# A planner that keeps an account of the engines' queues, and attention by query tile of both key heads

## The chip, the cores and the metric

The kernel runs on one core of one Trainium2 chip. The metric is the device time of one execution in microseconds (us), the median of the runs. Times in the trace are counted from the start of the span, the first instruction of the program in the profile.

## What is computed

The reference is the trunk of an encoder with two layers, in float32. Two sequences go through it with the same weights: the prompt (512 tokens, width 1024) and the sample (256 tokens).

```python
def mixer(h, lp, rope):
    z = h @ lp["w_mix_in"]
    ...
    o_lru = rglru_mixer(xb, yb, lp)
    o_rwkv = rwkv_mixer(zr, lp)
    o_att = attention(q, k, v, lp["attn_q_norm"], lp["attn_k_norm"], rope)
    o = jnp.concatenate([o_lru, o_rwkv, o_att], axis=-1).astype(h.dtype)
    return o @ lp["w_mix_out"]

def layer(x, c, lp, rope):
    mod = (jax.nn.silu(c) @ lp["w_ada"] + lp["b_ada"])[:, None, :]
    sh1, sc1, g1, sh2, sc2, g2, sh3, sc3, g3 = jnp.split(mod, N_MOD, axis=-1)
    h = rmsnorm(x, lp["norm_g"][0]) * (1 + sc1) + sh1
    x = x + 0.5 * g1 * swiglu(h, lp["ffn_w_in"][0], lp["ffn_w_out"][0])
    h = rmsnorm(x, lp["norm_g"][1]) * (1 + sc2) + sh2
    x = x + g2 * mixer(h, lp, rope)
    h = rmsnorm(x, lp["norm_g"][2]) * (1 + sc3) + sh3
    x = x + 0.5 * g3 * swiglu(h, lp["ffn_w_in"][1], lp["ffn_w_out"][1])
    return x
```

Attention has six query heads on two key heads (three query heads each), with 64 numbers a head. For every key head and each of its query heads it computes the scores q times k, a softmax over all tokens, and the product with v.

## The kernel before

Activations lie transposed, features on the partitions and tokens along the free axis. A token block is the whole sequence: 512 columns for the prompt, 256 for the sample. So the same matmul has a moving operand of 512 columns for the one and 256 for the other, and by that a row of the trace tells whose it is.

The dense work is the two feed-forward blocks of each layer and the mixer's two projections. Their weights come by DMA (`wr`), are split by ScalarE and VectorE into a high part `wh` (L270) and a rest `wl` (L271), and every product is three matmuls: `wh` with the high part of the activation, `wh` with its rest, `wl` with its high part (`mm3`). Names of their outputs: `pg` and `pu` (gate and up of the prompt), `pb` (both, of the sample), `ops` (the second matmul of the block, and `wmo`, the mixer's output projection, with `xo` as its input), `mip` (the mixer's input projection).

The small work is the rest. `ssp` is a norm's sum. Attention: `S` (scores), `ptp` (transposes of the probabilities P), `avp` (product with v). The recurrent mixer: `gps`. The RWKV mixer, for one pair of heads after the other: `up` and `ap` (low-rank gates), `kkp` and `bp` (sums over a head), `scps` (scores in chunks, from `AR`, `BK` and `B`), `btps` and `vtps` (transposes), then four levels of `yps` and `dps` (an inverse, in blocks of 32), `u0p`, the chunk recurrence `zps`, `saps`, `stps`, and the output `ywp`, `yp`, `gp`. `adaps` is the modulation. Many of these use a part of the 128 by 128 array, and a row of the trace says which: 64*128 is a half of the rows, 128*64 a half of the columns. A float32 matmul is two records in the trace (two passes), a transpose and a dense matmul are one.

Only TensorE's order is set by the kernel; the other engines' order comes from the framework. The planner is `Sched`. Each sequence's layers are a dense thread, a generator; attention, the recurrent mixer, RWKV and the modulation are small threads. A thread issues its instructions up to a `yield`. Each matmul moves the planner's clock `t` on by a fixed cost (512 columns divided by 2.4 GHz, and so on). What the thread yields is the time after which its next step may be issued, and that is a number written by hand for each place and each of the two sequences, in the table `LAT`:

```python
LAT = {... 'PREP': (5.0, 8.2), 'OP': (1.47, 0.82), ... 'A2': (2.0, 2.1), ... 'R3': (0.68, 0.99), 'R4': (1.8, 6.2), ...}
```

`step` sets `th.ready = self.t + r`. `run` takes a small thread that is ready, if the debt of small work allows it, else the dense thread of the lowest `prio`. In RWKV, `R3` stands between `yps` and `dps` and `R4` between `dps` and the next `yps`; `OP` and `PREP` stand in the preparation from `up` to `scps`. A dense thread yields 0.0 every two of its steps along the contraction (`EV`), so it is always ready, its inputs and weights or not.

An attention unit is (j, qt, hh): one of three query heads, one tile of 128 queries, one of the two key heads. Head `hh` lies on partitions 64 * hh to 64 * hh + 63. `stA` issues one `S` of 128 queries by all keys, and the softmax on VectorE and ScalarE. `stB` issues the transposes of P and the copy to PT, `stC` the product with v into the half `hh` of `avp`. A round of the loop issues `stA` of unit u, `stC` of u - 2 and `stB` of u - 1, then yields `A2`.

## Time and profile before

| | us |
|---|---|
| median of 3 runs (3454.62 to 3456.97) | 3456.47 |
| the profiled execution, its own time | 3462.16 |
| its span | 3459.2 |
| TensorE busy | 3341.5 |
| VectorE busy | 2003.2 |
| ScalarE busy | 1448.2 |
| GpSimd busy | 512.1 |

The span reaches from the first to the last instruction. The difference of 3.0 us from the profiled execution's time lies around it. Busy times are unions of an engine's records, and the end of a matmul's record is modelled, so consecutive records overlap; what a matmul costs in a stream is the distance of the starts.

### The profile page before, as it was taken

To read this page: it belongs to the slowest core of one execution; us is meant where nothing else is said; L and a number is where in the kernel's file an instruction comes from. 1 tells how busy PE (TensorE), PEld (TensorE's weight loads), DVE (VectorE), ACT (ScalarE), POOL (GpSimd) and SP (SyncE) were. 2 spreads that over 40 slices of the span, in tenths; PEclk is the share of its full clock that TensorE was granted. 3 is DMA by queue.
4 is the path that set the end of the run, shared out by engine and by line. 5 is a ranking of instruction groups with operands and counts; after the bars stand their busy time and mean duration, and the time that the engine had idled before them with its cause. 6 is when DMAs were issued, how large, how long until landed. Compare 5 with 4: busy or idle time off the path is not lost. (4 is left out here: it accounts for less than half of the span.)

```text
span 3459.2 us, 69173 instructions
## 1 busy us (share of the span) xinstructions
PE 3341.5 (97%) x28052; PEld 2734.0 (79%) x28052; DVE 2003.2 (58%) x3973; ACT 1448.2 (42%) x2730; POOL 512.1 (15%) x659
## 2 busy tenths in 40 slices
PE   7999999999899899999999999999899999999999
PEld 5777776678877777888888876788789978778899
DVE  4433365775776745546333476667557776446466
ACT  3322243644346433434333346534345564334354
POOL 1100020212221211111000111212211111111010
PEclk9999999999999999999999999999899999999999
DMA  7666674133342222423332331233245533223455
GB/s 276 219 206 208 203 270 145 57 104 113 100 153 93 83 80 83 132 90 119 92 98 86 119 114 62 79 110 102 82 161 164 179 106 108 63 91 125 138 177 161
DMA packets 151630, 445.80 MB, mean 129 GB/s; under 512 B 16912, under 2 KB 20752, under 8 KB 151312
## 3 DMA queue, kind: packets, MB, share of 16 engines
q1 hardware_dynamic: 151312, 441.39, 40.2%
q8 instruction: 220, 3.60, 0.4%
q14 instruction: 98, 0.80, 0.1%
HBM read 427.17 MB, written 14.16 MB: 128 GB/s over the span
## 5 line engine op out<-in xcount | busy, mean ns | idle before, releaser
L270 ACT ACTIVATE wh<-wr 128x512 fp32r<-128x512 f32 (+1 forms) x1368 | 816.6, 602 | 1572.1 <-PE ops L148 485.5
L271 DVE TENSOR_TENSOR wl<-wr,wh 128x512 fp32r<-128x512 f32 (+1 forms) x1368 | 907.3, 668 | 800.4 <-ACT wh L270 769.8
L148 PE MATMUL ops<-an,wh 128*128 128x512 f32 (+1 forms) x2816 | 717.8, 345 | 19.3 <-ACT an L351 7.3
L148 PEld LDWEIGHTS ops<-an,wh 128*128 128x128 f32 x2816 | 480.1, 190 | 99.1 <-issue 13.5
L148 PE MATMUL pb<-xn,wh 128*128 128x256 f32 x2816 | 525.1, 287 | 0.5 <-issue 0.5
L148 PE MATMUL ops<-an,wl 128*128 128x512 f32 (+1 forms) x1408 | 477.2, 339 | 0.1
L148 PE MATMUL pg<-xn,wh 128*128 128x512 f32 x1408 | 449.5, 400 | 7.8 <-ACT xn L417 5.9
L148 PEld LDWEIGHTS pb<-xn,wh 128*128 128x128 f32 x2816 | 433.6, 189 | 19.2 <-issue 11.2
L148 PE MATMUL pu<-xn,wh 128*128 128x512 f32 x1408 | 447.4, 399 | 0.0
L352 POOL TENSOR_TENSOR an<-sg,an 128x512 fp32r<-128x512 f32 (+1 forms) x176 | 192.3, 1093 | 1674.0 <-ACT an L351 1613.0
L148 PE MATMUL pb<-xn,wl 128*128 128x256 f32 x1408 | 396.4, 282 | 4.8 <-DVE wl L271 3.8
L431 DVE SCALAR_TENSOR_TENSOR x<-ops,gat,x 128x256 f32<-128x256 f32 (+1 forms) x352 | 215.8, 614 | 196.0 <-PE ops L148 190.6
L148 PE MATMUL mip<-xn,wh 128*128 128x512 f32 (+1 forms) x1216 | 314.2, 348 | 9.3 <-DVE f L583 2.9
L148 PEld LDWEIGHTS pg<-xn,wh 128*128 128x128 f32 x1408 | 260.1, 188 | 75.6 <-ACT xn L417 6.5
L148 PEld LDWEIGHTS pu<-xn,wh 128*128 128x128 f32 x1408 | 260.1, 188 | 65.5 <-issue 6.6
L148 PEld LDWEIGHTS ops<-an,wl 128*128 128x128 f32 x1408 | 267.0, 190 | 31.6 <-DVE wl L271 0.3
L148 PE MATMUL pg<-xn,wl 128*128 128x512 f32 x704 | 277.4, 394 | 0.0
L148 PE MATMUL pu<-xn,wl 128*128 128x512 f32 x704 | 276.8, 393 | 0.0
L148 PEld LDWEIGHTS pb<-xn,wl 128*128 128x128 f32 x1408 | 265.9, 189 | 6.0 <-DVE wl L271 4.8
L148 PEld LDWEIGHTS mip<-xn,wh 128*128 128x128 f32 x1216 | 208.2, 192 | 48.9 <-issue 12.3
L148 PE MATMUL mip<-xn,wl 128*128 128x512 f32 (+1 forms) x608 | 207.2, 341 | 0.0
L148 PEld LDWEIGHTS pg<-xn,wl 128*128 128x128 f32 x704 | 132.9, 189 | 30.7
(257 smaller groups left out, 3738.5 us busy)
## 6 DMA issues: line engine op xcount, KB each, us to landing
wr<-in_wfi_dram SPq DMA_DIRECT2D x352, 512.0 KB, 3.6
adaw<-in_wada_dram SPq DMA_DIRECT2D x128, 512.0 KB, 4.4
wr<-in_wfo_dram SPq DMA_DIRECT2D x192, 256.0 KB, 2.7
wr<-in_wfo_dram SPq DMA_DIRECT2D x128, 320.0 KB, 2.9
wr<-in_wmi_dram SPq DMA_DIRECT2D x76, 512.0 KB, 3.6
wr<-in_wmo_dram SPq DMA_DIRECT2D x32, 512.0 KB, 3.5
adaw<-in_wadh_dram SPq DMA_DIRECT2D x32, 256.0 KB, 5.2
xsp<-x SPq DMA_DIRECT2D x8, 512.0 KB, 3.6
```

What stands on the lines that cost most here:

```text
L148: PE.matmul(out, lhsT, rhs, start=start, stop=stop, skip_group_check=True)
L270: A.activation(out=hi[:, :n], in_=raw, func=AF.Copy)
L271: V.tensor_tensor(out=lo[:, :n], in0=raw, in1=hi[:, :n].bitcast(F32), op=ALU.subtract)
L352: eng.tensor_tensor(out=lo, in0=src, in1=hi.bitcast(F32), op=ALU.subtract)
L431: V.scalar_tensor_tensor(out=q.x[m], in0=ps, scalar=gat[l][:, i, m, q.i:q.i + 1], in1=q.x[m], op0=ALU.mult, op1=ALU.add)
```

## The change

The change puts an account of the engines' queues in place of the table. VectorE, ScalarE and GpSimd are wrapped (`Engine`): each instruction that the kernel issues there also enters `Model.op`, which gives it a duration by engine, operation and length, starts it once its inputs are written and its output buffer is free, and puts it into the first hole of that engine's queue that holds it (`place`). A matmul waits in the account for its operands, costs 0.4531 ns a column if dense, and 0.1 us more where dense and small work change places (`SWITCH`). The DMA of a weight takes 3.4 us (`DMAT`). A thread that yields a number over zero is now ready 0.05 us after the last instruction of its step ends in the account; one that yields `At(t)` is ready at `t`. A dense thread yields before every second step of the contraction until two inputs (and, at each fourth, the weights) are due. Small threads also wait until the account has a PSUM buffer free for them.

Attention becomes one unit for each (j, qt), with both key heads: two `S` one after the other on different rows of the array, both transposes, and the products with v alternating between the halves of the columns. Scores, transposes and product now are three steps with a yield behind each. The pool `small` has 7 buffers instead of 5, since a unit holds two P. P is overwritten by its transpose instead of a tile PT.

```diff
+SWITCH = 0.1
+DMAT = 3.4
...
+        self.mo.step_last = 0.0
...
+        elif isinstance(r, At):
+            th.ready = r.t
+        elif r > 0 and self.mo.step_last > 0:
+            th.ready = self.mo.step_last + 0.05
...
+            bank = self.mo.bank("m")
+            now = [th for th in act if max(th.ready, 0.0 if th.dense else bank) <= self.t + 1e-9]
             if not now:
-                self.t = min(th.ready for th in act)
+                self.t = min(max(th.ready, 0.0 if th.dense else bank) for th in act)
...
+class Engine:
+
+    def __init__(self, real, m, kind):
+        self.real, self.m, self.kind, self.iv = real, m, kind, []
+
+    def __getattr__(self, name):
+        call = getattr(self.real, name)
+
+        def run(*args, **kw):
+            r = call(*args, **kw)
+            aps = [a for a in args if hasattr(a, "dtype") and hasattr(a, "shape")]
+            outs = [kw[k] for k in ("out", "accum_out") if kw.get(k) is not None]
+            ins = [v for k, v in kw.items() if k not in ("out", "accum_out") and hasattr(v, "dtype") and hasattr(v, "shape")]
+            if "out" not in kw:
+                outs, aps = outs + aps[:1], aps[1:]
+            self.m.op(self, name, outs, ins + aps, kw)
+            return r
+
+        return run
+
+    def place(self, t0, dur):
+        iv = self.iv
+        k = len(iv)
+        while k > 0 and iv[k - 1][1] > t0:
+            k -= 1
+        s = t0
+        while k < len(iv) and iv[k][0] < s + dur:
+            s = max(s, iv[k][1])
+            k += 1
+        iv.insert(k, (s, s + dur))
+        if len(iv) > 400:
+            del iv[:200]
+        return s + dur
...
+    def op(self, e, name, outs, ins, kw):
+        n = 1
+        for a in outs[:1] + ins:
+            z = 1
+            for d in list(a.shape)[1:]:
+                z *= d
+            n = max(n, z)
+        t0 = self.ready(*ins)
+        for a in outs:
+            t0 = max(t0, self.free.get(self.keys(a)[0][0], 0.0))
+        if e.kind == "V":
+            if name == "tensor_tensor_scan":
+                d, lag = 0.1 + 2.15e-3 * n, 0.08
+            elif name == "tensor_scalar":
+                d, lag = 0.1 + 0.66e-3 * n, 0.08
+            elif name == "scalar_tensor_tensor":
+                d, lag = 0.1 + 1.08e-3 * n, 0.08
+            else:
+                d, lag = 0.08 + 1.03e-3 * n, 0.08
+            lag += 0.03
+        elif e.kind == "A":
+            d, lag = 0.11 + 0.83e-3 * n, 0.1
+            if kw.get("accum_out") is not None:
+                d += 0.2
+        else:
+            d, lag = (0.03 + 1.2e-3 * n if name == "memset" else 0.15 + (2.7e-3 if name == "tensor_scalar" else 2.05e-3) * n), 0.06
+        t = e.place(t0 + 0.06, d) + lag
+        for a in outs:
+            for k in self.keys(a):
+                self.w[k] = max(self.w.get(k, 0.0), t) if name != "memset" else max(self.w.get(k, 0.0), t)
+        for a in ins + outs:
+            nm = self.keys(a)[0][0]
+            r = self.r.get(nm, 0.0)
+            self.r[nm] = t if r >= 1e9 else max(r, t)
+        self.step_last = max(self.step_last, t)
+        return t
...
+    def mm(self, out, ins, cost, old):
+        t = self.sch.t
+        need = max(self.ready(*ins), self.free.get(self.keys(out)[0][0], 0.0))
+        if need > t + 0.02:
+            self.stalls.append((t, need - t, out.tensor.name, [a.tensor.name for a in ins if self.ready(a) >= need - 1e-6]))
+            t = need
+        dense = ins[1].dtype == F32R
+        if dense != self.dense:
+            t += SWITCH
+            self.dense = dense
+        t += cost
+        self.sch.t = t
+        for k in self.keys(out):
+            self.w[k] = t + 0.14
+        for a in ins:
+            nm = self.keys(a)[0][0]
+            self.r[nm] = max(self.r.get(nm, 0.0), t)
+        self.r[self.keys(out)[0][0]] = 1e9
...
+    def bank(self, tag):
+        names = self.ring.get(tag, [])
+        t = min((self.r.get(z, 1e9) for z in names), default=0.0)
+        return 0.0 if t >= 1e9 or len(names) < 4 else t
...
+    V, A, G, PE = Engine(nc.vector, mo, "V"), Engine(nc.scalar, mo, "A"), Engine(nc.gpsimd, mo, "G"), nc.tensor
...
-    sm = ctx.enter_context(tc.tile_pool(name="small", bufs=5))
+    sm = ctx.enter_context(tc.tile_pool(name="small", bufs=7))
...
+        if cost is None:
+            if rhs.dtype == F32R:
+                cost = (n * 0.4531 if n >= 256 else 213) * 1e-3
+            else:
+                conc = 1.0
+                if m <= 32:
+                    conc = 4.0
+                elif m <= 64:
+                    conc = 2.0
+                cost = max(4 * max(n, m) * 0.4453 / conc, 33.0) * 1e-3
+        mo.mm(out, (lhsT, rhs), cost, old)
...
             if k % 4 == 0:
+                wfill(q, look(q) + 1)
+                yield At(mo.ready(*q.wq[0], *xs[k], *xs[min(k + 1, nk - 1)]) if k else
+                         max(mo.ready(*q.wq[0], *xs[0], *xs[min(1, nk - 1)]), mo.free.get(out.tensor.name if hasattr(out, "tensor") else out.name, 0.0)))
                 wh, wl = wget(q)
+            elif k % every == 0:
+                yield At(mo.ready(*xs[k], *xs[min(k + 1, nk - 1)]))
             c = (k % 4) * 128
             for i, (a, b) in enumerate(((wh, xh), (wh, xl), (wl, xh))):
                 mm(out, a[:, c:c + 128], b, start=(k == 0 and i == 0), stop=(k == nk - 1 and i == 2))
-            if k % every == every - 1:
-                yield 0.0
...
-        yield LAT["A1"][q.i]
-        units = [(j, qt, hh) for j in range(3) for qt in range(nt) for hh in range(2)]
+        yield At(mo.ready(kr, vt, *M.qs[0:3]))
+        units = [(j, qt) for j in range(3) for qt in range(nt)]
         st = {}
 
-        def stA(u):
-            j, qt, hh = units[u]
-            b0, c0 = 64 * hh, qt * 128
-            S = sbank(n, name="S")
-            mm(S, M.qs[j][b0:b0 + 64, c0:c0 + 128], kr[b0:b0 + 64, :])
-            mx = tn(1, name="mx")
-            V.tensor_reduce(out=mx, in_=S, axis=AX.X, op=ALU.max)
-            c = (j * nt + qt) * 2 + hh
-            nb = tn(1, name="nb")
-            V.scalar_tensor_tensor(out=nb, in0=mx, scalar=-1.0, in1=rq[:, c:c + 1], op0=ALU.mult, op1=ALU.mult)
-            Pm = small(n, name="P")
-            ssum = tn(1, name="ssum")
-            A.activation(out=Pm, in_=S, func=AF.Exp, bias=nb, scale=rq[:, c:c + 1], accum_out=ssum)
-            ri = tn(1, name="ri")
-            V.reciprocal(out=ri, in_=ssum)
-            V.tensor_scalar(Pm, Pm, ri, None, ALU.mult)
+        def scores(u):
+            j, qt = units[u]
+            c0 = qt * 128
+            S = [sbank(n, name="S") for hh in range(2)]
+            for hh in range(2):
+                b0 = 64 * hh
+                mm(S[hh], M.qs[j][b0:b0 + 64, c0:c0 + 128], kr[b0:b0 + 64, :], cost=n * 1.25e-3)
+            nb, ss, Pm = tn(2, name="nb"), tn(2, name="ssum"), []
+            for hh in range(2):
+                V.tensor_reduce(out=nb[:, hh:hh + 1], in_=S[hh], axis=AX.X, op=ALU.max)
+            c = (j * nt + qt) * 2
+            V.scalar_tensor_tensor(out=nb, in0=nb, scalar=-1.0, in1=rq[:, c:c + 2], op0=ALU.mult, op1=ALU.mult)
+            for hh in range(2):
+                Pm.append(small(n, name="P"))
+                A.activation(out=Pm[hh], in_=S[hh], func=AF.Exp, bias=nb[:, hh:hh + 1], scale=rq[:, c + hh:c + hh + 1],
+                             accum_out=ss[:, hh:hh + 1])
+            ri = tn(2, name="ri")
+            V.reciprocal(out=ri, in_=ss)
+            for hh in range(2):
+                V.tensor_scalar(Pm[hh], Pm[hh], ri[:, hh:hh + 1], None, ALU.mult)
             st[u] = Pm
 
-        def stB(u):
-            Pm = st[u]
-            ptp = sbank(n, name="ptp")
-            for kt in range(nt):
-                trp(ptp[:, kt * 128:kt * 128 + 128], Pm[:, kt * 128:kt * 128 + 128], ident)
-            PT = small(n, name="PT")
-            A.activation(out=PT, in_=ptp, func=AF.Copy)
-            st[u] = PT
-
-        def stC(u):
-            j, qt, hh = units[u]
-            b0, c0 = 64 * hh, qt * 128
-            if hh == 0:
-                st["o"] = sbank(128, name="avp")
-            o = st["o"]
+        def turn(u):
+            ptp = [sbank(n, name="ptp") for hh in range(2)]
+            for hh in range(2):
+                for kt in range(nt):
+                    trp(ptp[hh][:, kt * 128:kt * 128 + 128], st[u][hh][:, kt * 128:kt * 128 + 128], ident)
+                A.activation(out=st[u][hh], in_=ptp[hh], func=AF.Copy)
+
+        def values(u):
+            j, qt = units[u]
+            o = sbank(128, name="avp")
             PT = st.pop(u)
             for kt in range(nt):
-                mm(o[b0:b0 + 64, :], vt[:, kt * 128 + b0:kt * 128 + b0 + 64], PT[:, kt * 128:kt * 128 + 128],
-                   start=(kt == 0), stop=(kt == nt - 1))
-            if hh == 1:
-                A.activation(out=M.oa[j][:, c0:c0 + 128], in_=o, func=AF.Copy)
+                for hh in range(2):
+                    b0 = 64 * hh
+                    mm(o[b0:b0 + 64, :], vt[:, kt * 128 + b0:kt * 128 + b0 + 64], PT[hh][:, kt * 128:kt * 128 + 128],
+                       start=(kt == 0), stop=(kt == nt - 1))
+            A.activation(out=M.oa[j][:, qt * 128:qt * 128 + 128], in_=o, func=AF.Copy)
 
         nu = len(units)
         for u in range(nu + 2):
             if u < nu:
-                stA(u)
+                scores(u)
+                yield At(mo.ready(*(list(st[u - 1]) if u else [kr])))
+            if 1 <= u <= nu:
+                turn(u - 1)
+                yield At(mo.ready(*(list(st[u - 2]) if u > 1 else [kr])))
             if u >= 2:
-                stC(u - 2)
-            if 1 <= u <= nu:
-                stB(u - 1)
-            yield LAT["A2"][q.i]
+                values(u - 2)
+                yield 0.0
```

TensorE's order in the prompt's attention of the first layer, before. `mip` is the prompt's own input projection.

```order
L148 MATMUL S<-qr 128x512
L148 MATMUL avp<-PT,sqz 64x128 x4
L163 MATMUL ptp<-cs,P 128x128 x4
L148 MATMUL mip<-xn,wh 128x512 x2
L148 MATMUL mip<-xn,wl 128x512
L148 MATMUL mip<-xn,wh 128x512 x2
L148 MATMUL mip<-xn,wl 128x512
L148 MATMUL adaps<-adaw,sc 32x256 x8
L148 MATMUL S<-qr 128x512
L148 MATMUL avp<-PT,sqz 64x128 x4
L163 MATMUL ptp<-cs,P 128x128 x4
L148 MATMUL mip<-xn,wh 128x512 x2
```

Each visit had one `S`, the `avp` of one head and four transposes. The same stretch now:

```order
L309 MATMUL S<-qr 128x512 x2
L309 MATMUL mip<-xn,wh 128x512 x2
L309 MATMUL mip<-xn,wl 128x512
L309 MATMUL mip<-xn,wh 128x512 x2
L309 MATMUL mip<-xn,wl 128x512
L326 MATMUL ptp<-cs,P 128x128 x8
L309 MATMUL avp<-P,sqz 64x128 x8
L309 MATMUL mip<-xn,wh 128x512 x2
L309 MATMUL mip<-xn,wl 128x512
L309 MATMUL mip<-xn,wh 128x512 x2
L309 MATMUL mip<-xn,wl 128x512
L309 MATMUL S<-qr 128x512 x2
```

Now two `S` stand together, and eight transposes and both heads' `avp` (the alternation isn't in the rows) stand four dense rows (six matmuls) later.

TensorE's order at the prompt's norm behind the first layer's `wmo`, before; `gps` and `mip` with 256 columns are the sample's, 120 such `mip` follow in all.

```order
L148 MATMUL ops<-xo,wh 128x512 x2
L148 MATMUL ops<-xo,wl 128x512
L148 MATMUL gps<-xc,gw 64x256 x8
L148 MATMUL ssp<-acc,cs 128x512
L148 MATMUL mip<-xn,wh 128x256 x2
L148 MATMUL mip<-xn,wl 128x256
```

The norm's `ssp` came ahead of dense matmuls of the sample. The same place now:

```order
L309 MATMUL up<-f,lw 128x256
L309 MATMUL ap<-f,lw 128x256
L309 MATMUL up<-f,lw 128x256
L309 MATMUL ssp<-acc,cs 128x512
L309 MATMUL kkp<-ksq,cs 128x256
L309 MATMUL bp<-kb,cs 128x256
L309 MATMUL scps<-AR,BK 128x128
L309 MATMUL scps<-AR,B_12310 128x128
...
L309 MATMUL pg<-xn,wh 128x512 x2
L309 MATMUL pg<-xn,wl 128x512
```

The sample's `mip` are all ahead of it. The sample's RWKV preparation, from `up` to eight `scps`, stands around `ssp` and ahead of the first `pg`.

TensorE's order in the sample's RWKV, two levels of the inverse, before: between `dps` and the next `yps` stand 30 dense matmuls of the prompt (20 rows, of which the first are shown).

```order
L148 MATMUL yps<-X,SC 32x32 x32
L148 MATMUL pu<-xn,wh 128x512 x2
L148 MATMUL pu<-xn,wl 128x512
L148 MATMUL pu<-xn,wh 128x512 x2
L148 MATMUL pu<-xn,wl 128x512
L148 MATMUL dps<-XT,Y 32x32 x32
L148 MATMUL pu<-xn,wh 128x512 x2
L148 MATMUL pu<-xn,wl 128x512
```

Now six stand in each place:

```order
L309 MATMUL yps<-X,SC 32x32 x32
L309 MATMUL pg<-xn,wh 128x512 x2
L309 MATMUL pg<-xn,wl 128x512
L309 MATMUL pg<-xn,wh 128x512 x2
L309 MATMUL pg<-xn,wl 128x512
L309 MATMUL dps<-XT,Y 32x32 x32
L309 MATMUL pu<-xn,wh 128x512 x2
L309 MATMUL pu<-xn,wl 128x512
L309 MATMUL pu<-xn,wh 128x512 x2
L309 MATMUL pu<-xn,wl 128x512
L309 MATMUL yps<-X,SC 32x32 x32
L309 MATMUL pu<-xn,wh 128x512 x2
```

## Rows read from the trace of the kernel before

**Rows 1.** The page: span, and busy us (share) xinstructions of each engine.

```profile
span 3459.2 us, 69173 instructions
...
PE 3341.5 (97%) x28052; PEld 2734.0 (79%) x28052; DVE 2003.2 (58%) x3973; ACT 1448.2 (42%) x2730; POOL 512.1 (15%) x659
```

**Rows 2.** Waits of PE: who waited for whom: total us, times, longest us.

```profile
PE ssp L148 <- DMA adaw<-in_wadh_dram: 14.0, 1, 14.0
PE scps L148 <- DVE BK L793: 13.8, 3, 6.1
PE ops L148 <- ACT an L351: 7.3, 5, 3.0
PE adaps L148 <- DMA adaw<-in_wadh_dram: 6.1, 1, 6.1
```

**Rows 3.** Windows: length, busy us of PE, PEld, DVE, ACT, POOL; granted clock, DMA.

```profile
700.00:742.00 42.00, 34.37 (x248) 30.38 (x248) 35.21 (x67) 21.46 (x41) 10.84 (x11) 0.95 0.44 137
1116.00:1147.30 31.30, 20.86 (x113) 16.70 (x112) 27.50 (x52) 19.73 (x33) 8.70 (x16) 0.78 0.28 93
```

**Rows 4.** Timeline of PE, one prompt attention unit: start us, us, instruction.

```profile
661.97 0.63 PE L148 MATMUL mip<-xn,wh 128*128 128x512 f32 x2
662.43 0.40 PE L148 MATMUL mip<-xn,wl 128*128 128x512 f32 x1
662.76 1.12 PE L148 MATMUL S<-qr 64*128 64x512 f32 x2
663.81 1.09 PE L148 MATMUL avp<-PT,sqz 128*64 128x128 f32 x8
664.83 0.66 PE L163 MATMUL ptp<-cs,P 128*128 128x128 f32 x4
665.24 0.71 PE L148 MATMUL mip<-xn,wh 128*128 128x512 f32 x2
665.80 0.39 PE L148 MATMUL mip<-xn,wl 128*128 128x512 f32 x1
```

**Rows 5.** Timeline of PE, one attention unit of the sample.

```profile
2821.70 0.70 PE L148 MATMUL S<-qr 64*128 64x256 f32 x2
2822.33 0.65 PE L148 MATMUL avp<-PT,sqz 128*64 128x128 f32 x4
2822.91 0.44 PE L163 MATMUL ptp<-cs,P 128*128 128x128 f32 x2
```

**Rows 6.** Timeline of PE, `up` and `ap` of the prompt.

```profile
703.33 0.69 PE L148 MATMUL up<-f,lw 64*128 64x512 f32 x1
703.33 0.69 PE L148 MATMUL ap<-f,lw 64*128 64x512 f32 x1
...
704.29 1.02 PE L148 MATMUL up<-f,lw 64*128 64x512 f32 x2
```

**Rows 7.** Timeline of PE: first of 16 `scps` records, and what follows them.

```profile
745.24 0.37 PE L148 MATMUL scps<-AR,BK 64*128 64x128 f32 x1
...
746.33 0.50 PE L148 MATMUL pb<-xn,wh 128*128 128x256 f32 x2
```

**Rows 8.** Timeline of PE: `ywp`, and what follows it.

```profile
838.41 2.08 PE L148 MATMUL ywp<-SAV,SC 128*64 128x64 f32 x64
840.42 0.51 PE L148 MATMUL pb<-xn,wh 128*128 128x256 f32 x2
```

**Rows 9.** Timeline of PE and DVE: the sample's RWKV preparation.

```profile
1156.07 0.48 PE L148 MATMUL up<-f,lw 64*128 64x256 f32 x1 [1.21 <-ACT f L588]
...
1175.60 0.76 DVE L793 TENSOR_TENSOR BK<-aa,cu 128x256 f32<-128x256 f32 x2 [0.59 <-POOL aa L790]
...
1187.38 0.37 PE L148 MATMUL scps<-AR,BK 64*128 64x128 f32 x1
```

**Rows 10.** Lines of DVE by form: busy us, mean ns of one, idle before.

```profile
L903 DVE STREAM_TRANSPOSE X<-XT 128x256 f32<-128x256 f32 x16 | 7.1, 445 | 0.5
L902 DVE TENSOR_TENSOR XT<-XT,dps 128x256 f32<-128x256 f32 x16 | 6.7, 421 | 16.0 <-PE dps L148 16.0
```

More of the change, by code (lines that the diff above doesn't have):

```diff
@@ L145, in dump, with load @@
             nc.sync.dma_start(out=dbg[name][:, q.o:q.o + q.n], in_=ap)
+    def load(out, src):
+        nc.sync.dma_start(out=out, in_=src)
+        mo.dma(out, src)
     def mm(out, lhsT, rhs, start=True, stop=True, cost=None):
@@ L296, in weight_raw @@
     def weight_raw(u):
-        raw = wsp.tile([128, 1024], F32, name="wr", tag="wr", bufs=NR)
-        nc.sync.dma_start(out=raw[:, :u.shape[-1]], in_=u)
+        raw = mo.alloc(wsp.tile([128, 1024], F32, name="wr", tag="wr", bufs=NR), "wr", NR)
+        load(raw[:, :u.shape[-1]], u)
         return raw
@@ L523, in mix_in @@
         rp = slot(q, "rp")
-        nc.sync.dma_start(out=rp, in_=rope[:, :, 0:n])
+        load(rp, rope[:, :, 0:n])
         for mt in range(19):
@@ L1043, in layer_thread @@
             for k in range(KD):
-                nc.sync.dma_start(out=q.x[k], in_=xT[k][:, q.o:q.o + q.n])
+                load(q.x[k], xT[k][:, q.o:q.o + q.n])
             nrm = Norm(q, 0, 0)
@@ L1099, in layer_thread @@
             for k in range(4):
-                nc.sync.dma_start(out=q.xd[k], in_=q.xsp[l][k])
+                load(q.xd[k], q.xsp[l][k])
             xo = []
@@ L1104, in layer_thread @@
                 od.append(slot(q, "ol"))
-                nc.sync.dma_start(out=od[k], in_=q.osp[l][k])
+                load(od[k], q.osp[l][k])
             for t in [od[k // 2][:, k % 2, :] for k in range(6)] + M.orw:
```

85 lines of the change are left out of this document (56 added, 29 removed).

## The prediction

> **What bounds the kernel now.** I read the page's busy table first. TensorE (PE) is busy 3341.5 of 3459.2 us, VectorE (DVE) 2003.2 [rows 1]. So about 118 us of the span is PE idle, and the rest of the time can only shrink if PE's own instructions take less time. A busy PE need not be a PE at its peak, so I went on to the timeline, where the distance from one start to the next says what a matmul really costs. A dense matmul of 512 columns costs 0.23 us (two take 0.46 us from start to start), whatever the 0.39 us of its own record says [rows 4]. That is steady work, and the change doesn't touch its amount. Two things are left to look at: the idle 118 us, and the small matmuls.
>
> The list of waits says where the idle time is [rows 2]. 14.0 + 6.1 = 20.1 us are the first loads, before the planner that the change rewrites has begun. The largest single item behind them is `scps` waiting three times for `BK`, 13.8 us, the longest 6.1 us: the RWKV preparation wasn't done when the fixed step times said it was. The rest is spread in pieces of a few us: `ops`, `pg` and `mip` waiting for a norm or an activation.
>
> The windows show why such waits exist [rows 3]. In 700:742 us, around the longest wait for `BK`, DVE is busy 35.2 of 42 us: with DVE that full, a chain of DVE steps is late because of what stands ahead of it in DVE's queue. In 1116:1147.3 us PE is busy only 20.9 of 31.3 us: the prompt's norm is running, and what the sample has to cover it runs out. The granted clock is 0.78 there, on average between the two levels, 2.4 GHz and 1.2 GHz, so such a gap also slows the matmuls behind it.
>
> **Part 1, attention: the term that rests on rows alone.** An attention unit of the prompt today is one visit of PE between dense matmuls [rows 4]. The dense matmul before it lasts 0.33 us instead of 0.23 (0.10 for entering), then S 1.05 us (662.76 to 663.81), `avp` 1.02, `ptp` 0.41, and the next two dense matmuls take 0.56 instead of 0.46 (0.10 for leaving): 2.68 us. There are 3 x 4 x 2 units in a layer and two layers, 48 in all: 128.6 us. For the sample S takes 0.63 and `avp` 0.58 us [rows 5]; two transposes fewer than the prompt's four, at 0.10 each, leave 0.21 us, and 0.20 goes for the visit: 1.62 us, 24 times: 38.9 us.
>
> After the change a unit is both heads. Does the array really do both halves at once? The kernel does that elsewhere. `up` and `ap` stand on rows 0 to 63 and 64 to 127, each with 512 columns: their first passes start together at 703.33, and the third matmul follows at 704.29, so the pair takes 0.96 us, less than one S takes alone now [rows 6]. I take 1.05 us for a pair of S, the same as one today with its switch to another shape. At 256 columns I take 0.63 in the same way. For `avp` the nearest row of the same length is a visit of `scps`: 16 records of 128 columns, halves alternating, in 1.09 us from 745.24 to 746.33 [rows 7], where `avp` today needs 1.02 us for 8. That is two row halves; `avp` has two column halves. Those are in `ywp`: 64 records of 64 columns in 2.01 us [rows 8]. At half of what a `ptp` of 128 columns takes (0.41/4 us) they would need 3.3 us one after the other, so the halves overlap there too. I take 1.09 us for the prompt's eight pairs of records, 0.65 for the sample's four. `ptp` stays as it is: at most 0.85 us for eight, 0.41 for four.
>
> The order shows two visits for most pairs (S; then `ptp` with `avp`), 0.40 us. A pair of prompt units: 1.05 + 1.09 + 0.85 + 0.40 = 3.39 us against 2 x 2.68 = 5.36, saving 1.97, 24 times: 47 us. A pair of sample units: 0.63 + 0.65 + 0.41 + 0.40 = 2.09 against 3.24, saving 1.15, 12 times: 14 us. Sum **61 us**, and all of it is on PE's own path, since PE is saturated around attention. The merged small DVE operations (one `nb` and one `ri` for both heads) are worth nothing here, being hidden behind PE. Two maxima and two exponentials now follow one S, but `ptp` of that unit comes only after the next S, about three blocks of six dense matmuls (1.4 us each) and another unit's `ptp` and `avp`. Without that cover a pair would stall PE by some us.
>
> Bounds: if column halves didn't overlap, `avp` would cost 2.04 and 1.16 us and the saving falls by 24 x 0.95 + 12 x 0.51 = 29 us, to 32. Upwards little is left, for example 0.1 us a pair with S as short as `up` with `ap`.
>
> The Trainium skill bears on this ("TensorE: Matmul & The Clock Gate", Part 3, The mechanism): a weight load overlaps matmuls in flight only when its row group differs. Two column halves share their row groups, so by that rule `avp` would gain nothing, which is the 32 us above. `ywp` in [rows 8] speaks against it, so it is a rival with a small chance.
>
> **Part 2, the order by an account.** It adds no instruction. Counted in the two orders, PE's visits to small work go from 468 to 488, dearer by 20 x 0.20 = **4 us**. Dense matmuls, weight loads, weight splits and DMAs are the same in number; the DMA issues move only with their consumers. So this part acts through waits alone. I go through them by place.
>
> (a) RWKV preparation, from `up` to `scps`. In the prompt the four old covers are 198, 216, 219 and 216 sample matmuls of half the 512-column cost (0.115 us), 23 to 25 us, and three of the four stalled, 13.8 us in all [rows 2]. The new covers are 213, 204, 198 and 186: 25, 23, 23 and 21 us. That isn't more, so with DVE as full as [rows 3] shows I expect these waits to stay at about their present sum. For the sample, three of the four covers shrink from 28 to 31 us to 13 to 15 us. The chain itself, with today's pauses in it, runs from 1156.07 (`up`) to the end of `BK` at 1176.36: 20 us, while `scps` came at 1187.38 only [rows 9]. So the old order wasted nothing but distance there, and the new one is shorter than today's chain. The account issues its steps sooner, so I put 3 us a place, 9 us, with 0 and 6 a place as bounds.
>
> (b) The prompt's norm after the first layer's `wmo`. Today 120 matmuls of the sample's `mip` (14 us) follow `ssp`, and still 10.4 us are idle [rows 3]. In the new order they are spent before `ssp`, and `kkp`, `bp` and eight `scps` of the sample stand ahead of the first `pg`. The norm then shares its hole with the 20 us chain of [rows 9]: idle up to 20 us instead of 10.4, so +8, bounds 0 and +15.
>
> (c) The sample's `yps` and `dps` in RWKV. After `dps` come XT and X on DVE, 0.42 + 0.45 us [rows 10], covered by 30 dense matmuls (6.9 us) before and by 6 (1.4 us) now. A weight split ahead of them on DVE would end that cover. There are 32 such visits (two head pairs in two layers, four levels of `yps` and `dps` each); at a mean of 0.2 us: +6, bounds 0 and +20.
>
> (d) The other waits. Of the 118 us, 20 are the start, 13.8 are (a), 10 are (b). In the remaining 74 the account should help: dense matmuls now wait their turn until two inputs and the weights are due, and small work takes their place, or the other way round. Where both threads are empty nothing can. I take half, -37, with 0 and -74 as bounds, and 5 us for the clock that comes back with shorter gaps.
>
> Sum of waits: 9 + 8 + 6 - 37 - 5 = -19. Sum of all: -61 + 4 - 19 = -76. The profiled execution took 3462.2 us against a median of 3456.5, 0.2% apart, which is also about what a measurement of this kernel can tell from no change; its terms are carried over to the median. **Forecast 3381 us**, 2.2% faster.
>
> **Rivals.**
> 1. *The account is too tight* (slower). It releases a step 0.05 us after its modelled end and may fill holes in a queue that the engine, working in order, can't fill. For: (a) to (c), and the full DVE of [rows 3]. Against: S, `avp` and most waits of today lie where there is other work. It decides if the new waits eat all of the gain of attention, 57 us net, and 7 us for the bound of 0.2%: spread over the 237 visits of `yps`, `dps`, `zps`, `saps` and `stps`, a mean of 0.27 us each. At 0.4 us each, with the places of (a) and (b) at their upper bounds, it gives 3456 - 57 + 95 + 33 - 37 = 3490 us.
> 2. *The halves of `avp` don't overlap*: 3381 + 29 = 3410 us. Against it stands [rows 8].
> 3. *The waits nearly vanish*: (a) to (c) at their lower bounds and -74 with 13 us of clock: 3456 - 57 - 87 = 3312 us. For: 118 us of idle time for 97% busy. Against: the places where both threads are empty are in the new order too.
> 4. *The change doesn't do what it says*: the new order is as good as the old, but waits merely move, and together with a shorter attention they come out even. It needs +57 us of waits, the same as rival 1 at its threshold: within 0.2%.
>
> **How the numbers follow.** The forecast's case, with waits between -65 and +35 us, 0.74: 3335 to 3435. Rival 3 0.08, rival 2 0.05, rival 1 0.09, rival 4 0.04. Faster by over 0.2% is the forecast, 2 and 3: 0.87; within it 0.04; slower 0.09. The range 3330 to 3440 leaves out rivals 1, 3 and 4 and little else, about 2 in 10.
>
> **What would show it.** Right: two S records of each half starting within 0.01 us of each other, and a pair at about 1.05 us; `avp` with 16 records in about 1.1 us; attention's PE time down by some 60 us at the same clock; the idle time of PE between 70 and 130 us, with `scps` and the place between `ssp` and the first `pg` still in its list. Wrong: `avp` records still 0.13 us apart (rival 2); waits of `yps`, `dps`, `zps` and `saps` of tens of us (rival 1); idle time near 40 us (rival 3). Most likely to be wrong is (d), which rests on no single row.

## The result: 1.1% slower

The changed kernel takes 3494.99 us (median of 4 runs, 3486.44 to 3501.04) against 3456.72 (3454.62 to 3459.76) for the one before on the same chip: a ratio of 1.0108, 95% interval 1.0084 to 1.0132. The forecast was 3381. The profiled execution has a span of 3496.1 us. The page says at once where to look (rows as in [rows 1]):

```profile
span 3496.1 us, 69090 instructions
...
PE 3310.4 (95%) x28052; PEld 2722.2 (78%) x28052; DVE 2007.8 (57%) x3901; ACT 1437.2 (41%) x2730; POOL 518.1 (15%) x659
```

TensorE is busy for 31 us less, half of what the cheaper attention was to save, and the span is 37 us longer. PE's idle time has gone from 117.7 to 185.7 us. The waits of PE, beside [rows 2], say where it came in (total, times, longest):

```profile
PE scps L309 <- DVE BK L128: 67.0, 8, 23.3
PE yp L309 <- DVE yy L128: 18.8, 6, 6.8
PE ssp L309 <- DMA adaw<-in_wadh_dram: 14.2, 1, 14.2
...
PE avp L309 <- ACT P L128: 6.3, 6, 1.6
PE ptp L326 <- DVE P L128: 4.6, 3, 2.6
...
PE ops L309 <- ACT an L128: 4.3, 2, 2.7
```

(Every operation of VectorE, ScalarE and GpSimd now has the wrapper's line, L128, so one goes by tiles.) `scps` waits for `BK` 67.0 us instead of 13.8. Summed over all rows of the list by what waits, before and after: `scps` 15.2 and 68.2; `yp` 3.5 and 18.8; attention (`S`, `ptp`, `avp`) 3.7 and 16.3; the inverse and the state chain (`btps`, `yps`, `dps`, `zps`, `saps`, `stps`) 24.9 and 30.9; the dense matmuls (`ops`, `pg`, `pu`, `pb`, `mip`) **41.7 and 22.6**. The dense threads wait less under the account, the small chains more.

**Attention did what it should.** The timeline of PE in a prompt unit, now both heads, beside [rows 4]:

```profile
638.10 1.09 PE L309 MATMUL avp<-P,sqz 128*64 128x128 f32 x16
639.12 0.51 PE L309 MATMUL pb<-xn,wh 128*128 128x256 f32 x2
...
640.02 1.13 PE L309 MATMUL S<-qr 64*128 64x512 f32 x4
641.08 0.51 PE L309 MATMUL pb<-xn,wh 128*128 128x256 f32 x2
...
641.89 1.03 PE L326 MATMUL ptp<-cs,P 128*128 128x128 f32 x8
642.68 0.48 PE L309 MATMUL pb<-xn,wh 128*128 128x256 f32 x2
```

Read the distances of the starts: `avp` 1.02 us for 16 records, where [rows 4] has 1.02 for 8; `S` 1.06 us for both heads, where one head took 1.05; `ptp` 0.79. The records come in pairs: in the trace the two halves of `avp` start 0.007 us apart (638.097 and 638.104), and so do the two `S` (640.022 and 640.029). So the halves of the columns work side by side. By the Trainium skill ("TensorE: Matmul & The Clock Gate", Part 3, The mechanism) a weight load overlaps matmuls in flight only when its row group differs. The prediction's rival took from this that `avp` would gain nothing, 2.04 us for the 16 records; the trace differs. That rule speaks of weight loads alone, so the step to "no gain" was the prediction's own.

**The preparation of RWKV is where the time went.** For the prompt's first pair of heads, from `up` to the first `scps`, the windows (columns as in [rows 3]) of everything, and of the weight splits `wl` alone (PE, PEld, DVE; clock, DMA):

```profile
705.93:742.58 36.65, 28.98 (x225) 26.57 (x224) 34.05 (x58) 19.06 (x37) 13.47 (x11) 0.94 0.46 139
```

```profile
705.93:742.58 36.65, 19.98 (x72) 13.36 (x71) 17.88 (x21) 0.94 0.46 139
```

VectorE is busy 34.05 of 36.65 us, and 17.88 of that are 21 splits of the other sequence's weights, more than half. The chain of the preparation waits in that queue. The end of the stretch in the timeline:

```profile
735.97 1.28 DVE L128 SCALAR_TENSOR_TENSOR BK<-csum,cu 128x512 f32<-128x512 f32 x2
737.77 0.80 DVE L128 TENSOR_SCALAR aa<-aa,kah,ka 128x1024 f32<-128x1024 f32 x1
738.65 2.72 POOL L128 TENSOR_TENSOR aa<-aa,f 128x1024 f32<-128x1024 f32 x1 [3.76 <-DVE aa L128]
...
739.43 2.49 DVE L128 TENSOR_TENSOR wl<-wr,wh 128x512 fp32r<-128x512 f32 x1
741.84 1.28 DVE L128 TENSOR_TENSOR BK<-aa,cu 128x512 f32<-128x512 f32 x2
...
742.58 0.79 PE L309 MATMUL scps<-AR,BK 64*128 64x128 f32 x2 [7.67 <-DVE BK L128]
```

In all four prompt preparations the chain takes what it took before (36.1, 32.9, 35.9 and 35.2 us before, 36.6, 36.8, 37.6 and 34.7 after, `up` to `scps`). The account, in its own books while the order was made, had 28.7, 27.6, 27.1 and 25.5, and the order put the `scps` there. The rows above show where a part of the difference comes from. After the first pair of `BK` the chain still needs `aa` on VectorE, `aa` on GpSimd and the second pair of `BK`: 5.9 us on the chip, from 737.25 to 743.12. The books have 1.2 us for it, because they put both `aa` into holes 16 and 13 us before the planner's present, ahead of the `BK` that was issued first. The other three preparations show the same: 5.3 to 5.8 us on the chip, at most 1.2 in the books. That is 4 to 6 of the 12 to 13 us by which the last `BK`, counted from `up`, is later on the chip than in the books. (The split at 739.43 lies under the GpSimd `aa`, which `BK` needs anyway; it costs the chain at most 0.5 us.) PE's waits in these stretches went from 20.3 to 35.0 us. For the sample, whose `scps` start 20.0, 21.8 and 19.4 us behind `up`, three covers of 14 to 17 us left 9.5 us of waits. The fourth is the longest wait of all, at the prompt's norm:

```profile
1136.01 1.13 PE L309 MATMUL ssp<-acc,cs 128*128 128x512 f32 x2
1136.98 0.59 PE L309 MATMUL kkp<-ksq,cs 128*128 128x256 f32 x2
1137.41 0.59 PE L309 MATMUL bp<-kb,cs 128*128 128x256 f32 x2
1161.30 0.76 PE L309 MATMUL scps<-AR,BK 64*128 64x128 f32 x2 [23.30 <-DVE BK L128]
...
1145.22 1.41 DVE L128 SCALAR_TENSOR_TENSOR xn<-nx,mod,xn 128x512 fp32r<-128x512 f32 x2
```

Two tiles of `xn` are written by 1146.6, but the prompt's first `pg`, which reads them, stands behind `scps` in PE's queue. This wait isn't an error of the books: there too TensorE stands idle between `ssp` and `scps`, for 23.0 us, since no other thread was ready.

With the idle gaps the granted clock falls too. Around this wait, where PE is busy 1.20 of 24.50 us, its mean is 0.58 (columns as in [rows 3]):

```profile
1137.00:1161.50 24.50, 1.20 (x6) 0.78 (x5) 21.83 (x54) 8.67 (x16) 7.72 (x10) 0.58 0.01 3
```

The means of the two kernels, before first:

```profile
core 0: 3459.2 us, clock 0.986
```

```profile
core 0: 3496.1 us, clock 0.972
```

Since the clock has two levels, 1.2 and 2.4 GHz, these means are 2 x 0.014 x 3459 = 97 us and 2 x 0.028 x 3496 = 196 us at the lower one.

### The profile page after: what moved, and what is told of

Same layout as the page of the kernel before. It is cut to its first block, busy times and chain, and to the rows that moved or that the text cites. A ratio compares the mean times of both kernels' runs of the same rounds, so it can differ in the third digit from the quotient of the medians.

```text
span 3496.1 us, 69090 instructions
## 1 busy us (share of the span) xinstructions
PE 3310.4 (95%) x28052; PEld 2722.2 (78%) x28052; DVE 2007.8 (57%) x3901; ACT 1437.2 (41%) x2730; POOL 518.1 (15%) x659
## 5 line engine op out<-in xcount | busy, mean ns | idle before, releaser
L128 ACT ACTIVATE wh<-wr 128x512 fp32r<-128x512 f32 (+1 forms) x1368 | 814.8, 600 | 1625.7 <-PE ops L309 489.6
L128 DVE TENSOR_TENSOR wl<-wr,wh 128x512 fp32r<-128x512 f32 (+1 forms) x1368 | 921.0, 677 | 785.1 <-ACT wh L128 746.0
L128 POOL TENSOR_TENSOR an<-sg,an 128x512 fp32r<-128x512 f32 (+1 forms) x176 | 191.9, 1090 | 1747.7 <-ACT an L128 1679.0
L128 DVE SCALAR_TENSOR_TENSOR x<-ops,gat,x 128x512 f32<-128x512 f32 (+1 forms) x352 | 216.2, 615 | 226.6 <-PE ops L309 222.1
L309 PE MATMUL mip<-xn,wh 128*128 128x512 f32 (+1 forms) x1216 | 322.9, 355 | 10.7 <-ACT zp L128 3.5
L309 PEld LDWEIGHTS ops<-an,wl 128*128 128x128 f32 x1408 | 267.6, 190 | 34.7 <-DVE wl L128 2.6
L309 PEld LDWEIGHTS pg<-xn,wl 128*128 128x128 f32 x704 | 133.6, 190 | 31.4
```

What stands on the lines that cost most here:

```text
L128: r = call(*args, **kw)
L309: PE.matmul(out, lhsT, rhs, start=start, stop=stop, skip_group_check=True)
```

## The experiments

Theory: the new attention is worth its 61 us of PE time, and the account loses more, because it releases steps ahead of what VectorE's queue can do. Rivals: attention itself makes the waits; or 3495 us is one unlucky order. Ratios are to the kernel before on the same chip. Idle is the span minus PE busy; `scps` all its waits, in us. These two come from the one profiled execution, which for most kernels lies within some 4 us of the median. For att_only it is 6 us and for `both` 10 us quicker; for the kernel before it is 5, for `margin` 6 and for floor_inorder 9 us slower.

| kernel | us | ratio (95% interval) | idle | `scps` |
|---|---|---|---|---|
| the change | 3495.0 | 1.0108 (1.0084 to 1.0132) | 185.7 | 68.2 |
| att_only | 3433.6 | 0.9939 (0.9923 to 0.9956) | 148.6 | 10.1 |
| acct_only | 3543.7 | 1.0255 (1.0239 to 1.0270) | 160.2 | 48.4 |
| now | 3503.0 | 1.0133 (1.0118 to 1.0148) | 188.7 | 7.3 |
| inorder | 3442.5 | 0.9959 (0.9944 to 0.9974) | 149.2 | 16.4 |
| inorder_now | 3514.9 | 1.0168 (1.0152 to 1.0183) | 199.2 | 1.6 |
| inorder_dve | 3451.1 | 0.9985 (0.9976 to 0.9994) | 149.6 | 4.8 |
| hold | 3484.5 | 1.0086 (1.0069 to 1.0103) | 173.1 | 26.3 |
| margin | 3479.9 | 1.0066 (1.0048 to 1.0084) | 170.6 | 31.4 |
| both | 3438.1 | 0.9939 (0.9917 to 0.9961) | 141.7 | 7.0 |
| floor_prep | 3463.8 | 1.0023 (1.0010 to 1.0036) | 152.4 | 12.3 |
| floor_chain | 3483.2 | 1.0072 (1.0057 to 1.0087) | 166.8 | 42.5 |
| floor_inorder | 3436.2 | 0.9936 (0.9920 to 0.9953) | 139.3 | 10.0 |
| floor_oldatt | 3481.3 | 1.0066 (1.0051 to 1.0081) | 127.1 | 9.4 |
| att_long | 3456.2 | 0.9998 (0.9989 to 1.0008) | 166.0 | 10.3 |
| att_deep | 3427.4 | 0.9910 (0.9893 to 0.9926) | 129.4 | 8.3 |
| nudge_up | 3513.0 | 1.0157 (1.0139 to 1.0175) | 191.5 | 51.9 |
| nudge_down | 3506.4 | 1.0140 (1.0122 to 1.0158) | 181.9 | 43.5 |
| nudge_before | 3478.8 | 1.0061 (1.0045 to 1.0077) | 135.1 | 9.4 |

### The two parts apart

att_only is the planner of before with the new attention, all three pieces in one visit:

```
-            yield LAT["A2"][q.i]
+            yield 2 * LAT["A2"][q.i]
```

> The old planner and its table of step times, with the new attention unit alone (scores, values, transposes in one visit, and twice the old step time behind it). If attention gives the 61 us that the prediction summed, and if one visit for two heads saves some 40 visits of 0.2 us on top: 3456.7 - 61 - 8 = 3388 us, with PE's waits within 15 us of the 118 before. If the column halves of avp didn't overlap: 3417. If attention's gain were lost to waits whatever the planner: 3450.

acct_only is the planner of the change with the old attention (`stA`, `stB`, `stC`).

> The new planner with the old attention unit (one key head, one S, one avp half at a time; its step time is now the end of its last instruction in the account). If the two parts add up, the account costs 3495 - 3457 + 61 = 99 us: 3556 us, with the wait of scps for BK near 67 us. If the account is only bad together with the new attention (its waits are those of avp, ptp and S, 16 us in the changed kernel): 3540 or less, and the wait for BK is near 14 us.

The signs are opposite: attention alone gains 0.6%, the account alone loses 2.5%. So attention isn't the cause. acct_only lies between its two expectations, and of its 80 us of longer span only 42.5 are idle time: PE busy rises by 37.8 us with the same number of matmuls, at a clock of 0.974 against 0.986. Attention's own gain is a third of the 61 us: att_only missed its 3388 us by 46. PE busy falls by 64.6 us there (3341.5 to 3276.9), and 30.9 of that come back as idle time in the profiled execution. The waits of att_only:

```profile
PE ptp L163 <- ACT P L639: 23.0, 13, 3.6
...
PE scps L148 <- DVE BK L793: 9.5, 2, 6.5
```

Two kernels tried to get these 23 us. att_long gives a step three times the old time, and att_deep one more step between scores and transposes:

```
+            if u >= 3:
+                values(u - 3)
+            if 2 <= u <= nu + 1:
+                turn(u - 2)
```

> The planner of before with the new attention, its step time three times the old one (6.0 and 6.3 us) where the earlier kernel had twice. Theory 1 (under fixed step times the new attention's gain was eaten by the transposes' wait for the weights): the 23 us of ptp waits fall below 8 and the time is 3410 to 3420 us. Theory 2 (a longer attention only moves the RWKV behind it later and the waits there take the gain back): 3430 us or more.

> The planner of before with the new attention at twice the old step time, but the transposes of a query tile follow its scores by two steps in place of one, and the products with the values by three. Theory 1 (the 23 us of ptp waits came from probabilities that had one step and needed more): ptp waits fall below 4 us and the time is 3408 to 3420 us, against 3433.6 with one step. Theory 2 (the time that attention no longer takes on PE was cover for the other chains, which wait instead): ptp waits fall, but others grow by most of it, and the time stays above 3425.

att_long is no faster than the kernel before: the `ptp` waits stay at 22.6 us, and the waits of the dense matmuls grow from 38.8 to 57.0. Theory 1 fails there. In att_deep the waits of attention fall from 29.4 to 8.6 us and the idle time by 19, but the gain is only 6 us, as PE busy rises by as much as the idle time falls, 3276.9 to 3295.8. The time is that of theory 2, though not by its means: the other waits grew by 2 us in sum. By the distances of starts, 8 us of the longer PE busy lie in attention's own records and 10 in dense matmuls; why is open. It is the fastest kernel of the study, 0.9% ahead of the one before.

### Is it the account's queue?

`now` books no operation before the planner's present; `inorder` fills no hole in a queue, except with weight splits; `inorder_dve` does that on VectorE alone; `inorder_now` does `now` and `inorder`:

```
-        t0 = self.ready(*ins)
+        t0 = max(self.ready(*ins), self.sch.t)
```

```
+        if not holes:
+            t0 = max([t0] + [z[1] for z in iv])
```

> The changed kernel with one word more in the account: no instruction is booked before the planner's present time. In the changed kernel the weight splits wh and wl, half of VectorE's work, are booked 100 to 700 us in the past, so the queue that a preparation step sees is about half empty. Theory of the past: the prompt's four waits of scps for BK (7.8 to 9.6 us each) fall under 3 us, the sum for scps from 67 to under 35 (the place at the prompt's norm, 23 us, is not of this kind), and the time is 3440 us or less. Theory of the holes (the account fills holes that a queue in order can't fill): nothing changes by over 10 us, 3485 to 3505. Theory of the margin (0.05 us behind a step is too little everywhere): 3480 to 3500, since no margin is added.

> The changed kernel with queues in order: each instruction but the weight splits is booked behind everything that its queue holds; the splits may still fill holes of the past. Theory of the holes: the waits of scps for BK fall under 35 us and the time under 3450 us. Theory of the past: VectorE's present queue still lacks the splits, the prompt's four waits stay over 4 us each, and the time stays over 3465 us. Theory of the margin: as now, 3480 to 3500.

> Both alterations of the account at once: no filling of holes (but for the weight splits) and no operation booked ahead of the present. Theory 1 (each makes the account more like the engine's queue, and the more alike the better): at or below the 3442 us of the kernel without hole filling. Theory 2 (booking the splits in the present pushes the preparation so far back that chains run out of covering matmuls): near the 3503 us of the kernel that books in the present, with scps waits gone and yps, yp and mip waits in their place.

> The changed kernel without hole filling on VectorE's queue alone (weight splits still fill holes; ScalarE and GpSimd fill holes as in the change). Theory 1 (the waits of the change come from VectorE's modelled queue): near the 3442 us of the kernel without hole filling on any engine, at most 3455. Theory 2 (the other two engines' queues do it, or the gain of that kernel was a lucky order): 3475 or more.

`inorder` gives back 52 us, as its theory of the holes had it, and `inorder_dve` 44, as its theory 1: it is VectorE's queue that matters. What goes are the `scps` waits; `yp` stays (20.0 us over all its rows, 18.8 in the change). Two rows of `inorder_dve`:

```profile
PE yp L311 <- DVE yy L128: 13.1, 5, 5.2
...
PE scps L311 <- DVE BK L128: 3.9, 2, 2.2
```

`now` takes the `scps` waits away too, which fits bookings in the past as their source. But as a remedy it falls: it is 8 us slower than the change, and other waits take their place:

```profile
PE yps L309 <- DVE X L128: 24.3, 12, 7.2
PE yp L309 <- DVE yy L128: 15.3, 6, 4.4
...
PE adaps L309 <- DMA adaw<-in_wada_dram: 11.4, 8, 3.5
```

`inorder_now` is worse still, against theory 1. There `scps` waits 1.6 us, and the inverse and the state chain 62.2 instead of 30.9. The prompt's first preparation has 411 dense matmuls of the sample for cover there and 213 in the change, so the order spends on one chain what others then lack.

The books themselves show how far each account was off. The order of the change ends there 3301 us after TensorE's first step; the chip's span is 3496 us, and that step starts 14.2 us into it. `inorder` and `inorder_dve` have 3388 and 3387 in their books, where the spans are 3440 and 3448. `now` and `inorder_now` err the other way, 3538 and 3621 for spans of 3503 and 3516: there the account is too late. Common to `now`, `inorder` and `inorder_dve` is that a step of a chain, like `aa` above, is no longer booked ahead of what was issued before it. No run changes that alone.

`hold` keeps the account and waits 9.0 or 4.0 us longer before the scores; `margin` makes every release 0.5 us later:

```
-        yield LAT["PREP"][q.i]
+        yield At(mo.step_last + (9.0, 4.0)[q.i])
```

```
-            th.ready = self.mo.step_last + 0.05
+            th.ready = self.mo.step_last + 0.55
```

> The changed kernel, with one release altered: the last step before the RWKV scores waits 9.0 us (prompt) or 4.0 us (short sequence) past the modelled end of its operands, in place of 0.05 us; these are about the amounts by which the trace of the changed kernel shows the preparation longer than the account had it. Theory 1 (the waits at the scores are themselves the cost): of the 67 us of scps waits the 23 us one at the norm stay or go by the new order, the other 44 us fall below 12, and the time is about 3455 us. Theory 2 (the same queue delays every later release too, so a wait taken away here comes back at yps, yp or the norms): scps waits fall, but the sum of PE's idle time falls by less than 15 us and the time stays above 3480.

> The changed kernel, with every release by the account 0.55 us after the modelled end in place of 0.05. Theory 1 (releases are merely too tight): the short waits of up to some 2 us, about 50 us in all, mostly go, and the time is 3450 to 3460. Theory 2 (the account misses whole stretches of VectorE's queue): the scps waits of 8 to 10 us lose half a microsecond each, those on the scores other than the one at the norm stay above 35 us, and the time stays within 12 us of 3495, unless the new order happens to move the 23 us wait at the norm, which would take up to 23 us more off.

`hold` is the run against my first reading, and it goes to theory 2. It takes 42 us of `scps` waits away, and the time falls by 10. The waits moved:

```profile
PE scps L309 <- DVE BK L128: 24.2, 7, 6.4
...
PE ops L309 <- ACT an L128: 11.4, 3, 8.0
PE pg L309 <- ACT xn L128: 10.6, 3, 7.6
PE avp L309 <- ACT P L128: 9.2, 6, 2.7
```

So the 67 us in the list of waits weren't 67 us to be had. `margin` gave 15 us, and its list no longer has the 23 us wait at the norm, but one of 14.9 us of `yp` some 30 us later. Neither of its theories has this: the time is above theory 1's 3460 us, and the `scps` waits are 31.4 us, under theory 2's 35. A tight margin by itself is not the cause.

### The old step times as a floor

`both` releases at the later of the account's time and the old step time; floor_prep does so in the RWKV steps up to the scores alone, floor_chain in those behind, floor_inorder together with `inorder`, floor_oldatt with the old attention:

```
-            th.ready = self.mo.step_last + 0.05
+            th.ready = max(self.mo.step_last + 0.05, self.t + r)
```

> The changed kernel, but every release by the account comes at the later of two times: 0.05 us after the modelled end, and the old fixed step time after the present. Theory 1 (the old step times carry what the account lacks, the work queued ahead on VectorE and ScalarE): the scps waits fall below 25 us, PE's idle time falls by 30 us or more, and the time is 3430 to 3455 us. Theory 2 (a later release only moves the wait to the next chain, as with the hold before the scores): idle falls by less than 15 us and the time stays above 3475.

> The changed kernel, with the old fixed step time as a floor under the account's release in the twelve steps of the RWKV preparation alone (up to the scores). Theory 1 (what the account gets wrong is the preparation, whose eleven steps share VectorE with the weight splits): nearly all of what the floor everywhere gave back, 3435 to 3450 us, with scps waits below 15. Theory 2 (scps waits move on to yps, dps and yp, as when only the last step was held): 3475 us or more.

> The same floor in the RWKV steps behind the scores alone (the inversion, the state chain, the outputs). Theory 1 (the preparation is the cause): within 15 us of 3495, the scps waits still above 45. Theory 2 (the steps behind are): 3440 to 3460 us, with scps waits as in the change.

> Both remedies at once: the old step times as a floor everywhere, and no filling of holes but for the weight splits. Theory 1 (both repair the same thing, releases ahead of VectorE's queue, so the second has little left to repair): within 15 us of the 3438 us that the floor alone gave, or of 3442. Theory 2 (they repair different things): 3395 to 3415 us.

> The planner with the account and with the old step times as a floor, and the old attention. Theory 1 (with the releases repaired the account and the old step times are worth the same, and the gain of the floored kernel against the kernel before is the new attention): 3450 to 3475 us, 15 to 35 us above the floored kernel with the new attention. Theory 2 (the new attention still brings its full saving of TensorE time): 3485 to 3500 us, 50 to 60 us above it.

`both` gives back 57 us, as theory 1 had it, and lies below the kernel before. Its `scps` row:

```profile
PE scps L309 <- DVE BK L128: 4.5, 1, 4.5
```

Of the 57 us the preparation brings 31 and the steps behind 12; neither theory of floor_prep has that, and it isn't all of it. floor_chain is theory 1's in time, with `scps` waits just under its 45 us. floor_inorder is within 2 us of `both`: the floor and the queue in order repair one thing, not two. floor_oldatt is 43 us above `both`, between its two theories: that is the new attention's worth here. PE busy falls by 67.3 us between the two (3352.3 to 3285.0). floor_oldatt is also 23 us slower than the kernel before, so the account with the floor is still no better than the table alone.

### Orders drawn anew

Every edit of the planner draws another order. The debt that lets small steps ahead (0.6) was changed for that alone:

```
-SLACK = 0.6
+SLACK = 0.7
```

> The changed kernel with the debt that lets small steps run ahead of dense ones set to 0.7 us in place of 0.6: no cause is repaired, only the order drawn anew. Theory 1 (the account's releases are the cost, whatever the order): 3475 to 3510 us, scps waits above 40. Theory 2 (3495 us was one unlucky order among many, and a remedy's 30 to 57 us can be luck): 3460 us or less.

> The same with 0.5 us. Theory 1 (the account's releases are the cost, whatever the order): 3475 to 3510 us, scps waits above 40. Theory 2 (an unlucky order): 3460 us or less.

> The kernel before with 0.7 us in place of 0.6. Theory 1 (its step times make good orders in general): 3445 to 3470 us. Theory 2 (its step times fit one order alone, the one they were chosen for): 3480 us or more, as slow as the account.

The change isn't one unlucky order: two others are 11 and 18 us slower, with `scps` waits of 43.5 and 51.9 us. So 52 and 57 us are more than chance by these draws (theory 1, if with one draw 3 us above its range), while the 10 to 15 us of `hold`, `margin` and floor_chain are not told from it. The kernel before moves by 20 us, to just under where its theory 2 began, so its order was a good draw of its table, and att_only and att_deep are measured against that.

## Why the prediction was wrong

**Part 1, attention.** Right as a cost on PE: 61 us forecast, and PE busy falls by 64.6 (att_only), 68.9 (the change against acct_only) and 67.3 us (`both` against floor_oldatt). Rival 2 fell with the 1.02 us of `avp`. Wrong was "all of it is on PE's own path": in time the three pairs give 22, 49 and 43 us. The likely reason is that PE's work was also the cover of the other chains, which wait when there is less of it: idle time grows by 30.9, 25.5 and 14.6 us in the three pairs. No run tests it apart from the order.

**Part 2.** The visits, 487 for 488 forecast, are right.

(a) For the sample's three places 9 us were forecast and 9.5 came. For the prompt the step "I expect these waits to stay at about their present sum" failed. It counted the covers, which were alike, and took three stalls from the list; all PE waits between `up` and `scps` were 20.3 us before and are 35.0 now, with covers 9 us shorter in the trace (108.4 to 99.4 us of dense matmuls).

(b) The place was right and the size 23.3 us of idle time against 10.4: +13, where +8 was taken and +15 was the bound.

(c) +6 was forecast, and the waits of the inverse and the state chain grew by 6.0. That the two agree so well is luck: in nudge_down they are 24.1 us, less than before.

(d) **This is the term that failed**: "the account should help", -37 us in the other waits, and -5 for the clock. The waits that are neither (a), (b) nor (c) came to +25 us of idle time (68.0 in all, less 9.5 + 14.7 + 12.9 + 6.0). The help is there for the dense matmuls, whose waits fell by 19, part of which only moved to (b). But `yp` grew by 15 and attention by 13. In `inorder`, `inorder_dve` and `both`, which give the time back, the help is gone as well: the dense matmuls wait 41 us as before. And the clock got worse, by 99 us more at the lower level. By the distances of starts attention's own records take 56 us less (153.4 to 97.5), but the dense matmuls, the same in number, 13 us more and the other small work 12 more.

In sums: idle time was forecast to change by -14 us (9 + 8 + 6 - 37) and changed by +68; PE busy by -62 (-61 + 4 - 5) and changed by -31.

**What the runs put in its place** is rival 1, given 0.09: the account fills holes that the engine doesn't (both `aa` of the preparation), and is too early. Its price was 3490 us and the result 3495, but that nearness is luck: 95 us of its price were waits of the inverse and the state chain, which grew by 6. Its mechanism was half right. The 0.05 us alone are not it (`margin`). The modelled queue of VectorE is (`inorder_dve`, `both`). I had named the full VectorE of [rows 3] as the reason for today's waits, and then trusted the account to know of it. Not settled is how the loss divides into bookings in the past, filled holes, durations that ignore GpSimd (below) and the lower clock; the runs change these together with the order. And 23 of the 67 us, at the norm, the books had foreseen.

## What to carry to other kernels

Fixed step times that were fitted on the chip carry the queueing that nobody wrote down; an account that replaces them has to be held against the trace in the fullest stretch of each engine before its times release anything, or take the old times as a floor. A wait's size in the list is not its price: take one away and see whether the time falls, since a chain that comes later spends cover that another had. When cheaper PE work is also the cover of VectorE chains, don't count on all of it (here a third to three quarters came), and draw the planner's order anew once or twice before a gain of less than 20 us is believed.

## What the runs showed of the hardware

A split `wl` of 512 columns that meets no GpSimd work takes at most 0.70 us in the traces of before, the change, `both` and att_only (median 0.69 over 1006 of them in the change). Of the 113 that lie under GpSimd work for more than half their time in the change, 62 take no longer; the other 51 are late, up to 2.72 us, and the mean of all 113 is 0.96. The row at 739.43 above is such a one: it lasts 2.49 us and ends 0.55 us after GpSimd's `aa`. So do the other three that take over 2 us (0.548 or 0.549 us each): the split ends when GpSimd is done, and isn't merely slowed. Why 62 aren't held up isn't shown. That agrees with the Trainium skill ("SBUF — State Buffer", SBUF: two separate sides): VectorE with two SBUF inputs and GpSimd share a pair of ports that one of them holds for a whole instruction. At 113 x 0.27 us it is an estimate of 31 us of VectorE in the changed kernel. The kernel before has 17 us of the same, so it isn't new with the change; the account has no such term. No run here took it away.
